# A hybrid S5 / gated-DeltaNet encoder step: tables behind the first block, the second block's norm in two operations, the steps' tiles placed anew

## The chip, the core and the metric

The kernel runs on one NeuronCore of one Trainium2 chip. A core has five engines that run in parallel, each through its own list of instructions and strictly in that order: TensorE (PE, matrix products, with PEld for its weight loads), VectorE (DVE), ScalarE (ACT), GpSimd (POOL) and SyncE (SP). They wait for each other through semaphores. Transfers between HBM and the on-chip memory SBUF are issued by SP, ACT or POOL and carried out by 16 DMA engines. Products land in PSUM, a small memory of eight banks, from which ACT or DVE copies them out ("evicts" them).

The metric is the device time of one execution in microseconds (us); less is better.

## The reference

Two layers work on one prompt of 2048 rows and on eight sample streams of 16 rows each, 2176 rows of width 1024 in all. Each layer is a normalisation, a modulation from a conditioning vector `c`, a mixer, and a gated residual:

```python
cs = jax.nn.silu(c)
for i in range(DEPTH):
    mod = cs @ w_ada[i] + b_ada[i]
    shift, scale, gate = jnp.split(mod[:, None, :], 3, axis=-1)
    h = rms_norm(x, norm_g[i]) * (1.0 + scale) + shift
    out = s5_branch(h, ...) if i == 0 else gdn_branch(h, ...)
    x = x + gate * out
y = rms_norm(x, final_g)
```

The change lies in layer 0, the S5 mixer:

```python
proj = h @ w_in                        # 1024 -> 2048
u, z = jnp.split(proj, 2, axis=-1)
# 64 groups of 16 channels, each with 64 complex states:
#   x_t = Abar x_{t-1} + Bbar u_t,   y_t = Re(C x_t)
# Abar = exp(lambda * step), Bbar = (Abar - 1) / lambda * B
y = gelu(y + d * u)
y = y * sigmoid(y @ w_glu + b_glu) * silu(z)
out = y @ w_out
```

Everything is float32. To keep that precision on PE at a higher rate, an operand is split into a high half (rounded to the fp32r format) and a low half (the rest), and each product is made of three: high x high, high x low, low x high.

## The kernel before, in words

**Blocks.** Rows are held transposed: features on the 128 partitions, in 8 slices of 128, and rows as columns. The columns are cut into 8 blocks of 272 (256 of the prompt, 16 of the samples). The first phase takes each block through norm, modulation, split into halves (`hh`, `hl`) and the first half of `w_in`: 8 column tiles `cb`, each 8 slices x 3 = 24 products into one PSUM tile (`pd`), evicted by ACT (`ev`) and stored to `u_d`. The modulated block itself is stored to `h0_d`, because the second half of `w_in` is applied to it later.

**The first block.** At the start nothing is loaded yet, so the order is written out by hand. A wrapper `Engine` with `ordered = True` issues each instruction of an engine behind the one before it in the program; it is set for T (PE), V (DVE) and S (ACT) from line 378 to line 423, and for SY (SP). The loop over slices (385 to 408) makes, for slice `k`, the products that give its shift and scale (`first_mod`), splits two column tiles of the weights (`split_raw`), normalises the slice, adds the products of an earlier slice (`first_prod`) and scales the slice (`first_scale`). Behind the loop, lines 409 to 421, stand the products of slices 6 and 7, the square of the second block (`norm_sq(xt1, xsq)`), two evictions, the split of the weight tiles 6 and 7, the second block's norm and modulation (`apply_mod(1, ..., True)`), column tiles 6 and 7 of the first block, and the other evictions. `norm_sq` squares half a block on ACT and adds it up on DVE; `norm_r` sums over partitions with a product by a constant matrix (`ms`), takes the root on ACT and the reciprocal on DVE; `norm_mul` multiplies the whole block by it.

**Everything else is placed by a planner.** An instruction that is not ordered is put into its engine's list by the framework, which simulates the program and takes what is ready; `later(list)` and `tc.issue_after(...)` make it keep an instruction behind given ones on the same engine. `after` is the last DVE instruction of the hand-written part. Not ordered are the step coefficients on 32 columns (430 to 505: `dexp`, the sine, the repeated squarings `unit_square` in `transitions`, which also makes `abar`, `nr`, `ni`), the tables of the steps (`s5_tables`, in 8 parts, on POOL with some rows on DVE at lines 555 and 557, loads and stores on POOL's queue), and the rotation tables (`rot_factors`, `rot_table`, on DVE, stored through ACT's queue). Before the change `s5_tables` parts are issued in blocks 1 to 6 with no `later`, the rotation tables in blocks 0 to 5 behind `after`.

**The loop over blocks** (589 to 618) computes block `j` and, at `cb == 4`, modulates block `j + 1`, loads block `j + 2` and issues the tables that are due; at `cb == 7` it normalises block `j + 2`. Its products are ordered on PE only for `j == 1`.

**The steps.** The second phase (631 to 937) takes 16 steps, each for two of the state pairs, with the scan on DVE. Between them PE is filled with `z_block`: 24 products of the second half of `w_in`, evicted by ACT as `evz` out of two PSUM buffers. In each step `n` such blocks are issued (3 or 4), and behind the first of them ACT copies the states (`s5_states`). The tiles of the steps come from three memory pools, `b3`, `b2` and `b1`, opened in this order on the memory that the first phase leaves.

Of the kernel before, what the change touches and what calls it, by code (L numbers as in the profile page):

```python
# [10 lines left out]
F32 = mybir.dt.float32  # L11
# [24 lines left out]


PWO, BBO, BDO, CCO, SPW = 0, 54, 118, 246, 310
TABLES = {1: (0, 1), 2: (2,), 3: (3,), 4: (4, 5), 5: (6,), 6: (7,)}
NATT = [(0, 512), (512, 512), (1024, 384), (1408, 384), (1792, 384)]  # L40


# [12 lines left out]
def kernel(ctx: ExitStack, tc: tile.TileContext, I, O, upto="Z"):  # L55
# [156 lines left out]
    def ks(t, n=KC):  # L212
        return [t[:, k] for k in range(n)]
# [13 lines left out]
    def split_x(nm, xt, hf):  # L227
        a = hp.tile([P, 4, NCH], F32R, tag="hh", name=f"hh{nm}_{hf}")
        b = hp.tile([P, 4, NCH], F32R, tag="hl", name=f"hl{nm}_{hf}")
        spl["i"] = [S.copy(a, xt).ins, V.tensor_sub(b, xt, a.bitcast(F32)).ins]  # L230
        return ks(a, 4), ks(b, 4)

    with ExitStack() as pa:
# [11 lines left out]
            ld = SY.dma_start(xt, I["xT"][j])  # L245
            return xt, ld.ins

        def norm_sq(xt, sqs=None):
            acc = sp1.tile([P, 2, NCH], F32, tag="acc", name="acc")
            for hf in range(2):  # L250
                sq = sqs[:, 4 * hf:4 * hf + 4] if sqs else sp1.tile([P, 4, NCH], F32, tag="sq", name="sq")
                xh = xt[:, 4 * hf:4 * hf + 4]
                S.activation(sq, xh, AF.Square)
                V.tensor_add(sq[:, 0:2], sq[:, 0:2], sq[:, 2:4])
                V.tensor_add(acc[:, hf], sq[:, 0], sq[:, 1])
            return acc
# [16 lines left out]
        def norm_x(xt, fold=False):  # L273
            return norm_mul(xt, norm_r(norm_sq(xt), fold=fold))

        def apply_mod(j, xt, first=False):
            xs = xt[:, :, NPC:NCH].rearrange("p k (q h) -> p k q h", h=2)
            V.tensor_mul(xs, xs, bc(gs0[:, :, 1:9], 3, 2))
            V.tensor_add(xs, xs, bc(modT[:, 0:8, 1:9], 3, 2))
            hl = []  # L280
            for hf in range(2):
                k4 = range(4 * hf, 4 * hf + 4)
                if not first:
                    for k in k4:
                        xk = xt[:, k, 0:NPC]
                        S.activation(xk, xk, AF.Identity, scale=gs0[:, k, 0:1], bias=modT[:, k, 0:1])
                    hl.append(split_x(j, xt[:, 4 * hf:4 * hf + 4], hf))
                    continue
                a, b = (hp.tile([P, 4, NCH], F32R, tag=t, name=f"{t}{j}_{hf}") for t in ("hh", "hl"))
                S.copy(a[:, :, NPC:NCH], xt[:, 4 * hf:4 * hf + 4, NPC:NCH])  # L290
                for i, k in enumerate(k4):
                    xk = xt[:, k, 0:NPC]
                    S.activation(a[:, i, 0:NPC], xk, AF.Identity, scale=gs0[:, k, 0:1], bias=modT[:, k, 0:1])
                    V.tensor_scalar(xk, xk, gs0[:, k, 0:1], modT[:, k, 0:1], op0=ALU.mult, op1=ALU.add)
                V.tensor_sub(b, xt[:, 4 * hf:4 * hf + 4], a.bitcast(F32))
                hl.append((ks(a, 4), ks(b, 4)))
            (h0, l0), (h1, l1) = hl
            if j < 7:
                nc.scalar.dma_start(h0_d[j], xt)
            return h0 + h1, l0 + l1  # L300

        SY.ordered = True
        fold = sst.tile([P, 9], F32, name="fold")
# [81 lines left out]
        for k in range(KC):  # L385
            if k == 2:
                SY.dma_start(lsd, I["ls"])
                SY.dma_start(lre, I["lr"])
                SY.dma_start(lim, I["li"])
            nwt = load_mod(k + 1) if k < 7 else None  # L390
            if k == 6:
                xt1 = load_x(1)[0]
            mA = first_mod(k, wt)
            nraws = [load_raw(cb) for cb in ((2 * k + 2, 2 * k + 3) if k < 2 else (6, 7) if k == 6 else ())]
            for w in raws if k < 7 else ():
                split_raw(*w)
            V.tensor_mul(xcur[:, k], xcur[:, k], r0)
            if k == 1:
                first_prod(0)
            elif k == 2:  # L400
                first_prod(1, range(2))
            elif k == 3:
                first_prod(1, range(2, 6))
            elif k > 3:
                first_prod(k - 2)
            first_scale(k, mA)
            if k < 7:
                wt, raws = nwt, nraws
        first_prod(6)
        first_prod(7)  # L410
        acc1 = norm_sq(xt1, xsq)
        first_copy(0)
        first_copy(1)
        for w in raws:
            split_raw(*w)
        hnext = apply_mod(1, norm_mul(xt1, norm_r(acc1)), True)
        for cb in range(2, 8):
            if cb > 5:
                pd0 += [psd.tile([P, NCH], F32, tag="d", name=f"pd0_{cb}")]
                mm3(pd0[cb], ks(wu_hi[cb]), ks(wu_lo[cb]), *hcur)  # L420
            first_copy(cb)
        after = [V.last]
        T.ordered = V.ordered = S.ordered = False
        nc.scalar.dma_start(h0_d[0], xcur)
# [56 lines left out]
        def transitions():  # L481
            V.tensor_copy(gk[:, :, 0, :], un)
            for _ in range(3):
                unit_square(gk[:, :, 0, :], gk[:, :, 0, :])
            for lv in range(1, 7):
                unit_square(gk[:, :, lv, :], gk[:, :, lv - 1, :])
            V.tensor_mul(a8, gk[:, :, 0, :], bc(rN, 1, 2))

            V.tensor_mul(abar, un, bc(mag, 1, 2))
            e1, e2, den, xr = ta  # L490
            V.tensor_mul(e1, lre, lre)
            V.tensor_mul(e2, lim, lim)
            V.tensor_add(e1, e1, e2)
            V.reciprocal(den, e1)
            V.tensor_scalar(xr, abar[:, 0], -1.0, None, op0=ALU.add)
            V.tensor_mul(e1, xr, lre)
            V.tensor_mul(e2, abar[:, 1], lim)
            V.tensor_add(e1, e1, e2)
            V.tensor_mul(nr, e1, den)
            V.tensor_mul(e1, abar[:, 1], lre)  # L500
            V.tensor_mul(e2, xr, lim)
            V.tensor_sub(e1, e1, e2)
            V.tensor_mul(ni, e1, den)

        transitions()

        def s5_tables(part):

# [80 lines left out]
        for j in range(8):  # L589
            hh, hl = hcur  # L590
            T.ordered = j == 1
            for cb in range(8):
                if cb == 4:
                    if j < 7:
                        hcur = apply_mod(j + 1, xnext) if j else hnext
                    V.ordered = S.ordered = j == 0
                    if j < 6:
                        xn, xl = load_x(j + 2)
                        if j == 0:
                            xnext = norm_x(xn)  # L600
                    V.ordered = S.ordered = False
                    SY.ordered = False
                    for part in TABLES.get(j, ()):
                        s5_tables(part)
                    with later(after):
                        if j == 0:
                            rot_factors()
                        for i in range(3 * j, min(3 * j + 3, 16)):
                            rot_table(i)
                if j > 0:  # L610
                    ps = psd4.tile([P, NCH], F32, tag="d", name=f"pd{j}_{cb}")
                    i_ = mm3(ps, ks(wu_hi[cb]), ks(wu_lo[cb]), hh, hl)
                    store_u(j, cb, ps)
                if cb == 7 and 0 < j < 6:
                    xnext = norm_x(xn)
                if j > 1 and cb % 3 == 1:
                    with later([xl, i_]):
                        ada.pop(0)()
# [11 lines left out]

    with ExitStack() as pb:
        ps5 = pb.enter_context(ExitStack())
        b3 = ps5.enter_context(tc.tile_pool(reuse_waits="tile", name="b3", bufs=3))
        b2 = ps5.enter_context(tc.tile_pool(reuse_waits="tile", name="b2", bufs=2))
        b1 = ps5.enter_context(tc.tile_pool(reuse_waits="tile", name="b1", bufs=1))
        ps_t = pb.enter_context(tc.tile_pool(reuse_waits="tile", name="ps_t", bufs=1, space=PSUM))
        ps_b = pb.enter_context(tc.tile_pool(reuse_waits="tile", name="ps_b", bufs=1, space=PSUM))
        ps_y = pb.enter_context(tc.tile_pool(reuse_waits="tile", name="ps_y", bufs=2, space=PSUM))
# [178 lines left out]

        def s5_y(b, pl):
            toe, u, cx, x = toes[b], us[b], cxs[b], xss[b][0]
            y = b2.tile([P, 2, NCH], F32, tag="y", name=f"y{b}_{pl}")  # L820
            pys = [ps_y.tile([P, NCH], F32, tag="y", name=f"py{b}_{2 * pl + i}") for i in range(2)]
            for i in range(2):
                T.matmul(pys[i], lhsT=toe[:, 2 * pl + i], rhs=u[:, 2 * pl + i], start=True, stop=False)
# [61 lines left out]
        for b in range(16):  # L885
# [32 lines left out]
            n = 4 if b % 2 == 0 and b < 11 or b == 15 else 3  # L918
            for i in range(n):
                z_block()  # L920
                if i == 0:
                    s5_states(b, t, xo)
                if i == 1 and len(zh) < 14 and zst["n"] >= 8 * (len(zh) // 2):
                    next_half()
# [1329 lines left out]
```

## Time and profile before

| what | value |
|---|---|
| median of three runs | 2116.36 us (2115.76 to 2120.4) |
| the profiled execution, its own time | 2108.51 us |
| its span, first to last instruction | 2106.8 us |
| mean granted PE clock | 0.992 of full speed |
| PE busy | 2049.0 us, 97% |
| DVE busy | 1484.4 us, 70% |
| ACT busy | 1013.8 us, 48% |
| POOL busy | 489.5 us, 23% |
| HBM traffic | 168 GB/s over the span |

The profile is of one execution. Each row of a timeline gives the start and the duration of an instruction in us, its engine, its line in the kernel (L70 is the wrapper of the ordered instructions), the operation, the written and read tiles, and, in brackets, how long the engine had been idle before it and what released it. The granted clock is the share of PE's full speed that the hardware allowed in that stretch.

### The profile page before, as it was taken

What the parts mean: (1) busy time and instruction counts of PE and PEld (TensorE: products, weight loads), DVE (VectorE), ACT (ScalarE), POOL (GpSimd) and SP (SyncE); (2) the same over time, 40 slices, a digit from 0 to 9 for tenths busy, and PEclk for the clock granted to TensorE, in tenths of its full rate; (3) what the DMA queues carried; (4) which work ended last, traced back from release to release, by engine and by line L of the source; (5) the groups of instructions that cost most, each with busy time, mean ns of one, the idle gap of its engine ahead of it and who ended that gap; (6) DMA issues with size and microseconds to landing.
All of it is one profiled execution on the core that took longest, in us unless ns stands there. A gap on an engine that the chain in (4) does not pass through costs nothing.

```text
span 2106.8 us, 41346 instructions
## 1 busy us (share of the span) xinstructions
PE 2049.0 (97%) x15473; PEld 1826.3 (87%) x15473; DVE 1484.4 (70%) x3401; ACT 1013.8 (48%) x2426; POOL 489.5 (23%) x742
## 2 busy tenths in 40 slices
PE   7899999999999999999999999999999899999998
PEld 5798888888889999999888879899987688888886
DVE  7988558788667544556665669688556788888885
ACT  3544335555455444445665422342223656666663
POOL 3089210000113322221100010100011344444430
PEclk9899999999999999999999999999999999999999
DMA  7687846666477433326565212653455944444432
GB/s 290 253 291 282 288 148 203 193 188 194 138 246 253 137 110 110 114 92 243 153 198 172 80 54 75 165 149 103 137 169 198 302 148 136 132 138 150 149 115 71
DMA packets 318069, 356.34 MB, mean 169 GB/s; under 512 B 88906, under 2 KB 261466, under 8 KB 315052
## 3 DMA queue, kind: packets, MB, share of 16 engines
q1 hardware_dynamic: 186700, 242.62, 36.1%
q10 hardware_dynamic: 126944, 98.57, 14.2%
q0 software_dynamic: 4224, 12.51, 1.7%
q8 instruction: 122, 2.00, 0.4%
q14 instruction: 79, 0.65, 0.1%
HBM read 229.20 MB, written 124.41 MB: 168 GB/s over the span
## 4 chain that ended last, share of the span: by engine, by line
PE 82%; DVE 7%; DMA 6%; ACT 3%; issue 1%; POOL 1%; SPq 0%; ACTq 0%; DVEq 0%; POOLq 0%
PE pdz L70 8%; PE epo L70 7%; PE pc L152 5%; PE pc L153 5%; PE pc L154 5%; PE pz L154 3%; PE pz L153 3%; PE pz L152 3%; PE py L70 3%; PE po L152 3%; PE po L154 3%; PE po L153 3%; PE pd L152 2%; PE pd L154 2%; PE pd L153 2%; PE pg L154 2%
## 5 line engine op out<-in xcount | busy, mean ns | idle before, releaser
L152 PE MATMUL pc<-h1h,wdh 128*128 128x512 f32 (+1 forms) x600 | 216.5, 361 | 0.4 <-ACT pb L1549 0.4
L153 PE MATMUL pc<-h1l,wdh 128*128 128x384 f32 (+1 forms) x600 | 214.8, 358 | 0.2 <-POOL h1l L1500 0.2
L154 PE MATMUL pc<-h1h,wdl 128*128 128x384 f32 (+1 forms) x600 | 214.9, 358 | 0.0
L1560 DVE SCALAR_TENSOR_TENSOR ac<-pb,convw,ac 128x384 f32<-128x384 f32 (+3 forms) x288 | 163.6, 591 | 3.3
L152 PE MATMUL po<-gh,woh 128*128 128x272 f32 x512 | 145.3, 290 | 2.4 <-ACT gh L1084 1.7
L154 PE MATMUL po<-gh,wol 128*128 128x272 f32 x512 | 147.4, 289 | 0.0
L153 PE MATMUL po<-gl,woh 128*128 128x272 f32 x512 | 147.1, 289 | 0.2
L70 PE MATMUL pdz<-hhz,wzh 128*128 128x272 f32 x448 | 131.9, 294 | 4.4 <-ACT evz L70 4.4
L153 PE MATMUL pg<-yl,wgh 128*128 128x272 f32 x448 | 129.8, 290 | 0.0
L70 PE MATMUL pdz<-hhz,wzl 128*128 128x272 f32 x448 | 129.5, 289 | 0.0
L154 PE MATMUL pg<-yh,wgl 128*128 128x272 f32 x448 | 129.3, 289 | 0.0
L70 PE MATMUL pdz<-hlz,wzh 128*128 128x272 f32 x448 | 129.2, 288 | 0.0
L152 PE MATMUL pg<-yh,wgh 128*128 128x272 f32 x448 | 129.0, 288 | 0.0
L152 PEld LDWEIGHTS pc<-h1h,wdh 128*128 128x128 f32 x600 | 112.6, 188 | 12.7 <-issue 1.7
L153 PEld LDWEIGHTS pc<-h1l,wdh 128*128 128x128 f32 x600 | 112.7, 188 | 10.5 <-issue 0.8
L154 PEld LDWEIGHTS pc<-h1h,wdl 128*128 128x128 f32 x600 | 112.6, 188 | 10.1 <-issue 0.8
L152 PE MATMUL pd<-hh,wuh 128*128 128x272 f32 x384 | 112.1, 293 | 0.0
L70 PE MATMUL epo<-w2h,ohi 128*128 128x512 f32 x272 | 111.5, 410 | 0.0
L154 PE MATMUL pd<-hh,wul 128*128 128x272 f32 x384 | 110.8, 289 | 0.0
L153 PE MATMUL pd<-hl,wuh 128*128 128x272 f32 x384 | 110.1, 287 | 0.0
L70 PE MATMUL epo<-w2l,ohi 128*128 128x512 f32 x272 | 107.6, 395 | 1.8 <-DMA w2l<-w2l_d 1.7
L1081 POOL TENSOR_TENSOR zt<-zt,sz 128x272 f32<-128x272 f32 x64 | 61.3, 964 | 206.0 <-ACT sz L1080 205.1
(647 smaller groups left out, 6338.5 us busy)
## 6 DMA issues: line engine op xcount, KB each, us to landing
wa<-in_w_ada SPq DMA_DIRECT2D x32, 512.0 KB
wdr<-in_w_in SPq DMA_DIRECT2D x24, 512.0 KB
u_d<-ev ACTq DMA_DIRECT2D x64, 136.0 KB
u<-u_d SPq DMA_DIRECT2D x16, 544.0 KB
z_d<-evz ACTq DMA_DIRECT2D x64, 136.0 KB
y_d<-y ACTq DMA_DIRECT2D x32, 272.0 KB
zt<-z_d SPq DMA_DIRECT2D x64, 136.0 KB
xa<-in_xT SPq DMA_DIRECT2D x8, 1088.0 KB
```

Source lines behind the costliest of these rows:

```text
L70: i_ = f(*a, **kw)
L152: T.matmul(ps, lhsT=w_hi[k], rhs=x_hi[k], start=(k == 0), stop=False)
L153: T.matmul(ps, lhsT=w_hi[k], rhs=x_lo[k], start=False, stop=False)
L154: i_ = T.matmul(ps, lhsT=w_lo[k], rhs=x_hi[k], start=False, stop=(k == n - 1))
L1081: G.tensor_mul(zt, zt, sz)
L1560: V.scalar_tensor_tensor(o, src(j), convw[:, b, j:j + 1], o, op0=ALU.mult, op1=ALU.add)
```

## The change

Four things are done.

1. *Tables and coefficients.* `TABLES` puts the parts in pairs into blocks 2 to 5, and their issue, like that of the rotation factors and tables (one block later than before), stands under `later(after)`. The last part of `transitions` becomes `step_factors`, also under `later(after)`. The squarings stay where they were.
2. *The second block's norm.* Its square is made in the loop of the first block, one half in slice 6 and one in slice 7; ACT's table for the root is loaded ahead of it. The split of the weight tiles 6 and 7, the sum over partitions and the root come ahead of the last slice's products.
3. *Its modulation, in two operations.* `second_block` replaces the normalisation of the whole block and the scaling: one DVE operation multiplies by the reciprocal and by the scale, one ACT operation adds the shift and rounds to the high half, and one DVE operation adds the shift and subtracts the high half. ACT then adds the shift once more, in place, for the copy that is stored. Evictions stand between the halves, and the products of column tiles 6 and 7 ahead of it all.
4. *The steps.* Pool `b1` is opened ahead of `b3` and `b2`, the `y` tile moves into it, and in step 15 the copies of the states stand behind the second `z_block` instead of the first.

```diff
-TABLES = {1: (0, 1), 2: (2,), 3: (3,), 4: (4, 5), 5: (6,), 6: (7,)}
+TABLES = {2: (0, 1), 3: (2, 3), 4: (4, 5), 5: (6, 7)}
...
-        def norm_sq(xt, sqs=None):
-            acc = sp1.tile([P, 2, NCH], F32, tag="acc", name="acc")
-            for hf in range(2):
+        def norm_sq(xt, sqs=None, acc=None, part=range(2)):
+            acc = sp1.tile([P, 2, NCH], F32, tag="acc", name="acc") if acc is None else acc
+            for hf in part:
...
+        def second_block(xt, r, copies):
+            xs = xt[:, :, NPC:NCH].rearrange("p k (q h) -> p k q h", h=2)
+            V.tensor_mul(xs, xs, bc(r[:, NPC:NCH].rearrange("p (q h) -> p q h", h=2), 1, KC))
+            V.tensor_mul(xs, xs, bc(gs0[:, :, 1:9], 3, 2))
+            V.tensor_add(xs, xs, bc(modT[:, 0:8, 1:9], 3, 2))
+            a, b = ([hp.tile([P, 4, NCH], F32R, tag=t, name=f"{t}1_{hf}") for hf in range(2)] for t in ("hh", "hl"))
+            for hf in range(2):
+                for i in range(4):
+                    k = 4 * hf + i
+                    xk = xt[:, k, 0:NPC]
+                    V.scalar_tensor_tensor(xk, r[:, 0:NPC], gs0[:, k, 0:1], xk, op0=ALU.mult, op1=ALU.mult)
+                    S.activation(a[hf][:, i, 0:NPC], xk, AF.Identity, bias=modT[:, k, 0:1])
+                S.copy(a[hf][:, :, NPC:NCH], xt[:, 4 * hf:4 * hf + 4, NPC:NCH])
+                for cb in copies[hf]:
+                    first_copy(cb)
+            for hf in range(2):
+                for i in range(4):
+                    k = 4 * hf + i
+                    V.scalar_tensor_tensor(b[hf][:, i, 0:NPC], xt[:, k, 0:NPC], modT[:, k, 0:1],
+                                           a[hf][:, i, 0:NPC].bitcast(F32), op0=ALU.add, op1=ALU.subtract)
+                V.tensor_sub(b[hf][:, :, NPC:NCH], xt[:, 4 * hf:4 * hf + 4, NPC:NCH],
+                             a[hf][:, :, NPC:NCH].bitcast(F32))
+            for k in range(KC):
+                xk = xt[:, k, 0:NPC]
+                S.activation(xk, xk, AF.Identity, bias=modT[:, k, 0:1])
+            nc.scalar.dma_start(h0_d[1], xt)
+            return [ks(t[0], 4) + ks(t[1], 4) for t in (a, b)]
...
             V.tensor_mul(xcur[:, k], xcur[:, k], r0)
+            if k == 6:
+                S.preload_act_table_set("sqrt_and_others")
+            if k > 5:
+                acc1 = norm_sq(xt1, xsq, acc1 if k == 7 else None, (k - 6,))
...
+        for w in raws:
+            split_raw(*w)
         first_prod(6)
+        r1 = norm_r(acc1)
         first_prod(7)
-        acc1 = norm_sq(xt1, xsq)
         first_copy(0)
         first_copy(1)
-        for w in raws:
-            split_raw(*w)
-        hnext = apply_mod(1, norm_mul(xt1, norm_r(acc1)), True)
-        for cb in range(2, 8):
-            if cb > 5:
-                pd0 += [psd.tile([P, NCH], F32, tag="d", name=f"pd0_{cb}")]
-                mm3(pd0[cb], ks(wu_hi[cb]), ks(wu_lo[cb]), *hcur)
-            first_copy(cb)
+        for cb in range(6, 8):
+            pd0 += [psd.tile([P, NCH], F32, tag="d", name=f"pd0_{cb}")]
+            mm3(pd0[cb], ks(wu_hi[cb]), ks(wu_lo[cb]), *hcur)
+        hnext = second_block(xt1, r1, ((2, 3), (4, 5)))
+        first_copy(6)
+        first_copy(7)
         after = [V.last]
...
+        def step_factors():
             V.tensor_mul(abar, un, bc(mag, 1, 2))
...
         transitions()
+        with later(after):
+            step_factors()
...
-                    for part in TABLES.get(j, ()):
-                        s5_tables(part)
                     with later(after):
-                        if j == 0:
+                        for part in TABLES.get(j, ()):
+                            s5_tables(part)
+                        if j == 1:
                             rot_factors()
-                        for i in range(3 * j, min(3 * j + 3, 16)):
+                        for i in range(max(0, 3 * j - 3), min(3 * j, 16)):
                             rot_table(i)
...
+        b1 = ps5.enter_context(tc.tile_pool(reuse_waits="tile", name="b1", bufs=1))
         b3 = ps5.enter_context(tc.tile_pool(reuse_waits="tile", name="b3", bufs=3))
         b2 = ps5.enter_context(tc.tile_pool(reuse_waits="tile", name="b2", bufs=2))
-        b1 = ps5.enter_context(tc.tile_pool(reuse_waits="tile", name="b1", bufs=1))
...
-            y = b2.tile([P, 2, NCH], F32, tag="y", name=f"y{b}_{pl}")
+            y = b1.tile([P, 2, NCH], F32, tag="y", bufs=2, name=f"y{b}_{pl}")
...
-                if i == 0:
+                if i == b // 15:
                     s5_states(b, t, xo)
```

The branch of `apply_mod` that served the second block alone is removed with it.

More of the change, by code (lines that the diff above doesn't have):

```diff
@@ L274, in norm_x, with apply_mod @@
             return norm_mul(xt, norm_r(norm_sq(xt), fold=fold))
-        def apply_mod(j, xt, first=False):
+        def apply_mod(j, xt):
             xs = xt[:, :, NPC:NCH].rearrange("p k (q h) -> p k q h", h=2)
@@ L281, in apply_mod @@
             for hf in range(2):
[L282 to L291, printed above, removed]
+                for k in range(4 * hf, 4 * hf + 4):
                     xk = xt[:, k, 0:NPC]
[L293 to L296, printed above, removed]
+                    S.activation(xk, xk, AF.Identity, scale=gs0[:, k, 0:1], bias=modT[:, k, 0:1])
+                hl.append(split_x(j, xt[:, 4 * hf:4 * hf + 4], hf))
             (h0, l0), (h1, l1) = hl
```

## The prediction

> **What bounds the kernel now.** I read the page first, then the waits, then the timeline of each engine up to 140 us, and last the stretch round the sixteenth S5 step.
>
> ```profile
> span 2106.8 us, 41346 instructions
> PE 2049.0 (97%) x15473; PEld 1826.3 (87%) x15473; DVE 1484.4 (70%) x3401; ACT 1013.8 (48%) x2426; POOL 489.5 (23%) x742
> ```
>
> PE lacks only 2106.8 - 2049.0 = 57.8 us, so a change pays where PE waits or where its clock is down. The waits of PE, for the first 80 us and then from there to 560 us (total, times, longest):
>
> ```profile
> PE ms L70 <- DVE acc L70: 10.2, 3, 7.9
> PE pd L70 <- ACT ev L70: 4.7, 1, 4.7
> PE psc L70 <- DVE mA L70: 3.7, 2, 2.7
> ...
> PE pb L70 <- issue: 0.5, 1, 0.5
> PE pdz L70 <- ACT evz L70: 0.4, 1, 0.4
> ```
>
> The 7.9 us are the wait for the very first input. The other large ones fall between 47 and 77 us, where the first block of 272 columns ends and the second is made ready; from 80 to 560 us PE waits 0.9 us in all. PE's own rows (start, duration, in brackets the idle time before):
>
> ```profile
> 46.83 0.29 PE L70 MATMUL pd<-hl,wuh 128*128 128x272 f32 x1
> 46.95 0.28 PE L70 MATMUL pd<-hh,wul 128*128 128x272 f32 x1
> ...
> 77.05 0.59 PE L70 MATMUL pd<-hh,wuh 128*128 128x272 f32 x1 [4.70 <-ACT ev L70]
> ...
> 81.52 0.39 PE L70 MATMUL pd<-hl,wuh 128*128 128x272 f32 x1
> 81.75 0.29 PE L70 MATMUL pd<-hh,wul 128*128 128x272 f32 x1
> ```
>
> Before the stalls one product starts about 0.125 us after the last (46.95 - 46.83), behind them 0.227 us (81.75 - 81.52). So a stall is paid twice, as idle time and in clock. The stretches round the first stall show the same (busy time of PE, PEld, DVE, ACT, POOL, then granted clock, DMA share, GB/s):
>
> ```profile
> 44.00:48.00 4.00, 3.24 (x34) 2.52 (x26) 3.53 (x15) 0.60 (x1) 3.59 (x12) 1.00 0.01 2
> 48.00:52.00 4.00, 2.04 (x13) 2.04 (x14) 4.00 (x19) 0.43 (x2) 3.53 (x11) 0.88 0.01 2
> ```
>
> What PE waits for is DVE. DVE works in order, and table work that the steps want 200 us later stands in that order ahead of the second block and waits for its own buffers:
>
> ```profile
> 53.94 0.46 DVE L555 TENSOR_TENSOR ca<-sp 128x288 f32<-128x288 f32 x1 [1.75 <-DMA ca_d<-ca]
> ...
> 60.74 0.83 DVE L555 TENSOR_TENSOR ca<-sp 128x288 f32<-128x288 f32 x2 [2.09 <-DMA ca_d<-ca]
> ...
> 66.14 1.84 DVE L70 RECIPROCAL r<-r 128x272 f32<-128x272 f32 x1
> ...
> 73.25 0.41 DVE L70 TENSOR_SCALAR x<-x,gs,modT 128x256 f32<-128x256 f32 x1
> ```
>
> **The head, part by part.** First what PE must still do after 47.1 (46.95 + 0.125) before block 1 may start, at full clock: the scale product of slice 7 (0.51), slices 6 and 7 of the first block at 18 x 0.125 = 2.25 each, columns 6 and 7 at 48 x 0.125 = 6.0, and the norm product, 0.92 by the chain of waits (start, duration):
>
> ```profile
> 104.37 0.92 PE ms L70 x4
> 105.29 0.38 PE pd L152 x3
> ```
>
> The sum is 11.9, so block 1 can start at 59.0 at best, against 77.05. Whether DVE and ACT allow it is the real question. The rows for it, of the timelines and of the groups on DVE between 36 and 77 us:
>
> ```profile
> 43.28 0.51 PE L70 MATMUL psc<-fold,mA 128*128 128x9 f32 x4
> ...
> 55.54 1.10 ACT L70 ACTIVATE xsq<-x 128x1088 f32<-128x1088 f32 x1
> ...
> 57.37 0.72 DVE L70 TENSOR_TENSOR xsq<-xsq 128x544 f32<-128x544 f32 x1
> ...
> 60.12 1.28 ACT L70 ACT_TABLE_LOAD   x1
> ...
> 72.55 2.07 ACT L70 ACTIVATE hh<-x,modT,gs 128x256 fp32r<-128x256 f32 x4
> ```
>
> ```profile
> L555 DVE TENSOR_TENSOR cat<-sp 128x288 f32<-128x288 f32 x8 | 3.6, 453 | 1.1 <-POOL sp L454 1.1
> L557 DVE TENSOR_TENSOR ca<-ca,cat 128x288 f32<-128x288 f32 x8 | 3.6, 447 | 0.0
> L555 DVE TENSOR_TENSOR ca<-sp 128x288 f32<-128x288 f32 x8 | 3.4, 459 | 3.8 <-DMA ca_d<-ca 3.8
> ...
> L70 DVE TENSOR_TENSOR wul<-wr,wuh 128x1024 fp32r<-128x1024 f32 x2 | 2.4, 1219 | 0.0
> ```
>
> *The two halves of the second block's square* now stand in slices 6 and 7, each ahead of that slice's scaling: 1.10 on ACT, then about 1.1 on DVE (0.72, and a sum of half that size). Their input has landed, since the DMA share is 0.01 from 44 us on. The preloaded table (1.28) stands ahead of the first square, so ACT ends it near 43.7, and DVE takes slice 6's scales near 44.8 instead of 43.8. What is queued behind it on DVE is the low half and the copy that PE's next scale product reads; that copy is there by 46.4, and PE has other products until 47.1. The cover is about 0.7 us; if it is gone, PE stands by what is missing, up to the 2.2 of both halves.
>
> *Weights 6 and 7* are split ahead of the norm instead of after it (2.4 on DVE), ending near 52.7. Then come the reciprocal (1.84) until 54.5, three narrow operations (0.7 together) until 55.2, and eight fused multiplies of 256 columns. The trace has no fused operation of this shape. The scalar form took 0.41; at a pace of 0.33, as such rows overlap, eight are 2.7, and at the 0.453 of the two-tensor rows of 288 columns above, without overlap, 3.6. I take 2.7, since the elements are those of the 0.41 row.
>
> So the low halves begin near 58, and the first four are there at 59.5. ACT makes its eight high halves beside them at 0.51 each (2.07 for four), with four evictions between, until 60.6, just ahead of the low halves that read them. The eight more ACT passes for the stored copy (4.1 us) and its store then lie beside the 24 us of block 1's products; without that cover they would delay the next square by as much.
>
> *Fillers.* The squarings of the rotation (L463 to L474) are not put behind the first block. Four rounds of 11 passed between 47 and 77, one start 0.1 us after the other:
>
> ```profile
> 71.77 0.18 DVE L463 TENSOR_TENSOR sm<-gk 128x32 f32<-128x32 f32 x1
> 71.88 0.18 DVE L464 TENSOR_TENSOR sm<-gk 128x32 f32<-128x32 f32 x1
> ```
>
> In the 12 us that are left, 44 x 0.1 x 12/30 = 1.8 us. I put block 1's start at 61.0, between 59.0 and 64.3 (59.0 + all 4.4 of the fillers + 0.9 of slower multiplies): a gain of 77.05 - 61.0 = 16.0, between 12.7 and 18.0. Of the 20 slow products behind 77.05 (20 x 0.102 = 2.0) I keep 0.7, as a shorter stall remains: gain 1.3, bounds 0 and 2.0.
>
> [...]
>
> *The seam to block 2.* Its square started at 80.73 and its products at 105.29, 24.6 us later, with no idle time and nothing to spare:
>
> ```profile
> 80.73 1.11 ACT L70 ACTIVATE sq<-x 128x1088 f32<-128x1088 f32 x1
> ```
>
> Now it starts near 67, after the stored copy and two evictions. Block 1 ends near 61 + 24 + 1.9 (two norm products) = 86.9, and 67 + 24.6 = 91.6: a stall of up to 4.7. But the rotation tables that shared DVE with it, which was full (27.10 of 28 us, below), now stand a block later. I charge 1.0, bounds 0 and 4.7.
>
> **What moves.** The 24 table rows above (10.6 us on DVE), their four stores, the POOL operations and small loads that feed them go behind the first block, two parts to a block from the third on. The rotation tables go one block on, with their stores on ACT's queue. PE covers this if DVE has room:
>
> ```profile
> 77.00:105.00 28.00, 27.95 (x201) 27.67 (x201) 27.10 (x114) 16.60 (x31) 2.02 (x3) 0.92 0.72 264
> ...
> 133.00:161.00 28.00, 28.00 (x220) 25.16 (x212) 25.48 (x51) 11.54 (x24) 27.13 (x64) 1.00 0.84 279
> ```
>
> One part is 10.6 / 2 = 5.3 us of DVE. Cost 0, down to -10 (the first rival). The small loads that POOL no longer issues at the start: 0. The new order of the steps' memory pools: 0, since PE waits at their start only the 0.5 us above.
>
> **Step 15.** Its state copies go behind the second gate block on ACT:
>
> ```profile
> 557.86 0.39 ACT L70 COPY evz<-pdz 128x272 f32<-128x272 f32 x1 [2.27 <-PE pdz L70]
> ...
> 565.23 1.24 ACT L70 COPY xs<-xo 64x510 f32<-64x510 f32 x2 [0.45 <-DVE xo L70]
> ...
> 566.93 0.59 PE L70 MATMUL pdz<-hhz,wzh 128*128 128x272 f32 x1 [3.10 <-ACT evz L70]
> ```
>
> The second eviction can then run near 561 (557.86 and a block of 24 x 0.125), so the 3.10 go, and with them some twelve slow products (1.2). Late next is the third eviction, behind the copies until 566.9, when PE ends its fourth block anyhow. Gain 4.0 of 4.3; 0 at least, if the next phase's weights hold PE instead.
>
> **The sum** is made against the profiled execution (span 2106.8, 2108.51 with what lies around it): 16.0 + 1.3 - 1.0 + 4.0 = 20.3 less. The median shown, 2116.36, lies 7.85 above that execution; I carry the difference over: 2116.36 - 20.3 = 2096.0.
>
> **Rivals.** *Half is given back by DVE.* The seam costs 4.7 and 2.0 of clock, and two blocks with a part more overrun 28 us (25.48 + 5.3 = 30.8, 2.8 each): 20.3 + 1.0 - 6.7 - 5.6 = 9.0 gained, time 2107.4. For it: 27.10 of 28 busy. Against it: from 80 us on PE waited for none of this. [...]
>
> ```profile
> 139.93 2.29 POOL L454 TENSOR_TENSOR sp<-pt,pt 128x4 f32<-128x4 f32 x1
> ...
> 139.61 2.54 DVE L270 TENSOR_TENSOR x<-x,r 128x2176 f32<-128x2176 f32 x1
> ...
> 230.41 0.55 POOL L558 DMA_DIRECT2D ca_d<-ca  x1 [5.37 <-DVE ca L557]
> ```
>
> *The second block is not ready earlier after all.* The squares in slices 6 and 7 and the fillers hold up the first block by what they save, and only step 15 is left: 2112.4. Against it: DVE's own waits of 1.75 and 2.09 go with the tables. *Slower: norm products stand in PE's order ahead of late sums.* If one part's DVE rows (5.3) stand between a sum and its norm product, PE stands as long and loses 1.2 in clock, in blocks 2 to 5: 26 lost, time 2122. It decides from 20.3 / 4 = 5.1 us per block. For it: pairs of parts. Against it: the last store, at 230.41, is 55 us ahead of the steps, so table work can slip behind sums.
>
> **How the numbers follow.** Forecast 0.64, half given back 0.19, not ready earlier 0.09, slower 0.08. About 0.2% (4.2 us) is what can be told from no change: faster 0.83, same 0.09, slower 0.08. The best case is 18.0 + 2.0 + 4.3 = 24.3, time 2092; the three times shown before spread from 2115.76 to 2120.4, so I put the lower end 3 lower, at 2089. The upper end, 2109, lies just past the first rival. The forecast's own range is 2089 to 2102.
>
> **What would show it.** Right: block 1's first product near 61 us, clock 1.00 from 32 us on, no table row on DVE before it, no wait of 3.1 in step 15. Wrong: PE waiting for a norm sum or a low half after 86 us; DVE above 27 of 28 in three blocks running; PE idle at the start of the steps.

## The result, and the profile after

The changed kernel takes 2100.62 us (median of four runs, 2098.2 to 2104.91); the kernel before, beside it on the same chip, takes 2117.99 (2115.76 to 2120.4). The ratio is 0.992, interval 0.9897 to 0.9943: 17.4 us less, where 20.3 were forecast. The time forecast, 2096.0, is 4.6 below the one measured, inside the range of 2089 to 2109. One of the twelve timed runs of e2 below took 5103.11 us and is left out of its figures.

The two profiled executions don't show this difference in their spans: the one shown of before was shorter than all its timed runs, and the one of after the longest of four. So what follows compares stretches of the traces, not their ends. The page of the changed kernel gives its span:

```profile
span 2103.2 us, 41357 instructions
```

The waits of PE up to 110 us (total, times, longest):

```profile
PE ms L70 <- DVE acc L70: 8.4, 2, 8.1
PE pd L152 <- ACT hh L230: 3.4, 1, 3.4
PE pd L70 <- DVE hl L70: 2.8, 4, 2.0
PE ms L263 <- DVE acc L70: 1.7, 1, 1.7
...
PE psc L70 <- DVE mA L70: 1.2, 2, 1.0
PE pd L153 <- DVE hl L230: 0.6, 1, 0.6
```

The wait of 4.7 for an eviction is gone, and that for `mA` fell from 3.7 to 1.2. But three entries are new: for the sum of a norm (L263), and for the high and the low half of block 2 (L230); and the wait for a low half of block 1 has grown from 1.2 to 2.8. PE's own rows show where they stand (start, duration, in brackets the idle time before):

```profile
59.81 0.39 PE L70 MATMUL pd<-hh,wuh 128*128 128x272 f32 x1
62.23 0.39 PE L70 MATMUL pd<-hl,wuh 128*128 128x272 f32 x1 [2.03 <-DVE hl L70]
...
70.67 0.72 PE L263 MATMUL ms<-acc,onesd 128*128 128x272 f32 x2 [1.73 <-DVE acc L70]
...
89.62 1.08 PE L70 MATMUL ms<-acc,onesd 128*128 128x272 f32 x4
94.09 0.78 PE L152 MATMUL pd<-hh,wuh 128*128 128x272 f32 x4 [3.39 <-ACT hh L230]
```

Blocks are counted from 0, so block 1 is the second one. It begins at 59.81 with a single product; with the next at 62.23 it is as far as if it had started at 62.1, against 77.05 before. It ends at 89.6. Block 2 then comes 3.39 us late. By stretches (busy time of PE, PEld, DVE, ACT, POOL, then granted clock, DMA share, GB/s):

```profile
77.00:105.00 28.00, 23.99 (x162) 23.05 (x162) 28.00 (x80) 13.05 (x25) 3.51 (x9) 0.88 0.67 247
105.00:133.00 28.00, 28.00 (x222) 24.35 (x221) 18.34 (x38) 11.88 (x25) 20.11 (x54) 1.00 0.87 299
133.00:161.00 28.00, 28.00 (x220) 25.16 (x212) 24.26 (x53) 11.56 (x23) 20.77 (x50) 1.00 0.92 313
```

The stretch from 77 to 105 us ran at a full PE (27.95 of 28) before. Now DVE is full there (28.00), PE lacks 4.0 us, and the clock is down to 0.88. From 105 us on PE is full, and DVE has room. The norm of block 2 starts with its square on ACT; then come DVE's rows:

```profile
68.00 1.12 ACT L70 ACTIVATE sq<-x 128x1088 f32<-128x1088 f32 x1
...
71.71 1.57 DVE L579 TENSOR_TENSOR ca<-sp 128x288 f32<-128x288 f32 x4
...
73.81 0.72 DVE L70 TENSOR_TENSOR sq<-sq 128x544 f32<-128x544 f32 x1
74.46 0.46 DVE L581 TENSOR_TENSOR ca<-ca,cat 128x288 f32<-128x288 f32 x1
...
75.48 0.43 DVE L70 TENSOR_TENSOR acc<-sq 128x272 f32<-128x272 f32 x1
...
80.63 1.84 DVE L70 RECIPROCAL r<-r 128x272 f32<-128x272 f32 x1
```

The rows of `ca`, which the program issues in block 2, stand here during block 1, between the square, its sum and the reciprocal. In the steps, PE's waits between 300 and 600 us are now these and one of 0.3; before there were 4.4 for the gate blocks' evictions (`evz`, under `pdz`) and 1.3 ahead of `pg`:

```profile
PE pg L70 <- DVE wgl L140: 0.7, 1, 0.7
PE pg L70 <- ACT evz L70: 0.5, 1, 0.5
```

### The profile page after: what moved, and what is told of

Its sections match the earlier page's. It is cut to its first block, busy times and chain, and to the rows that moved or that the text cites. A ratio compares the mean times of both kernels' runs of the same rounds, so it can differ in the third digit from the quotient of the medians.

```text
span 2103.2 us, 41357 instructions
## 1 busy us (share of the span) xinstructions
PE 2047.4 (97%) x15473; PEld 1825.1 (87%) x15473; DVE 1483.6 (71%) x3409; ACT 1015.1 (48%) x2434; POOL 489.1 (23%) x742
## 4 chain that ended last, share of the span: by engine, by line
PE 85%; DVE 6%; DMA 5%; ACT 3%; issue 1%; POOL 0%; SPq 0%; ACTq 0%; DVEq 0%; POOLq 0%
PE pdz L70 8%; PE epo L70 7%; PE pc L152 5%; PE pc L153 5%; PE pc L154 5%; PE pz L154 3%; PE pz L153 3%; PE pz L152 3%; PE po L154 3%; PE py L70 3%; PE po L153 3%; PE po L152 3%; PE pd L152 2%; PE pg L154 2%; PE pg L152 2%; PE pg L153 2%
```

## The experiments

Each kernel is compared with the kernel before on the same chip. Beside the ratio, the table has landmarks of the trace in us, read off the view by tile, whose rows give the first and the last start of a group. For the changed kernel these rows are

```profile
L152 PE MATMUL pd<-hh,wuh x384: 282/288/428, 94.1 to 265.3; 128*128 128x272 f32 x192
```

```profile
L70 PE MATMUL pdz<-hh,wzh x64: 283/288/400, 266.0 to 297.4; 128*128 128x272 f32 x64
```

```profile
L70 PE MATMUL pg<-yh,wgh x64: 283/287/396, 576.4 to 601.6; 128*128 128x272 f32 x64
```

"Block 2" is the first start of the first, "end of blocks" the last start of the second, "steps" the distance from there to the first `pg`, with which the next phase begins.

| kernel | block 2 | end of blocks | steps | first `pg` | median, us | ratio to before, interval |
|---|---|---|---|---|---|---|
| before, as shown | 104.9 | 304.5 | 285.4 | 589.9 | 2117.99 | 1 |
| c0, before again | 105.8 | 305.4 | 286.8 | 592.2 | 2115.86 | 1.0004 (0.9989 to 1.0018) |
| after, as shown | 94.1 | 297.4 | 279.0 | 576.4 | 2100.62 | 0.992 (0.9897 to 0.9943) |
| c1, after again | 93.7 | 296.8 | 279.0 | 575.8 | 2099.04 | 0.9921 (0.9905 to 0.9937) |
| e1 | 90.8 | 291.1 | 278.8 | 569.9 | 2094.32 | 0.9903 (0.988 to 0.9925) |
| e2 | 87.7 | 309.5 | 278.3 | 587.8 | 2114.39 | 0.9987 (0.9971 to 1.0003) |
| e3 | 93.8 | 295.6 | 283.6 | 579.2 | 2106.04 | 0.9952 (0.9936 to 0.9968) |
| e4 | 102.5 | 303.0 | 279.0 | 582.0 | 2110.1 | 0.9972 (0.9957 to 0.9987) |
| e5 | 96.6 | 299.2 | 285.8 | 585.0 | 2112.71 | 0.9983 (0.9971 to 0.9994) |
| e6 | 86.9 | 286.7 | 278.9 | 565.6 | 2091.78 | 0.9886 (0.9867 to 0.9905) |
| e7 | 92.7 | 294.2 | 282.7 | 576.9 | 2107.44 | 0.9968 (0.9954 to 0.9982) |
| e8 | 105.0 | 304.6 | 283.2 | 587.8 | 2113.67 | 0.9988 (0.9978 to 0.9998) |
| e9 | 90.7 | 293.4 | 279.0 | 572.4 | 2101.12 | 0.9928 (0.991 to 0.9945) |

**c0 and c1: both kernels again.** No edit.

> The kernel before, unchanged, for a trace beside those of the others. The profile shown before is of an execution of 2108.51 us, while the timed ones took 2115.76 to 2120.4. Theory 1: the start is the same in every execution (block 1's first product near 77 us, PE's wait of 3.1 in step 15), and the 7 to 10 us between executions arise behind step 15, where weights come by DMA; then this trace has block 1 near 77 and its extra time behind 560 us. Rival: executions differ by an even stretch of everything, and every mark of this trace lies some 0.4% later.

> The changed kernel, unchanged. Forecast of the prediction: 20 us less than before, ratio 0.990. By the two traces at hand: block 1's products from 60 us, block 2's from 94 to 96 us, 11 us ahead of the kernel before at step 15's last products. Ratio 0.990 to 0.994. If only the profiled executions counted, 3.6 us less, 0.998.

The two executions of each kernel agree within 1 us up to the end of the blocks (e3 and e7, with the same code up to there as after and c1, widen that to 3.2). The two of before are 0.1 apart at the last high product of the steps' gate blocks (588.1 and 588.2), 2.3 at the first `pg`, and 6.6 at the end. Most of this scatter lies behind the first `pg`, where the change touches nothing. From there to the start of the kernel's last group of products the thirteen traces take 1507.4 to 1523.1 us. The three with the whole head of before (before, c0, e8) are the shortest there, with 1507.4 to 1512.0. The medians don't bear this out as an effect of the change: they fall by 17.4 us, and the traces show 15.8 up to the first `pg` (below). What makes this scatter isn't located; the landmarks before it carry the reading.

**e1: the tables, and the rotation's factors and tables, behind block 2's split** instead of behind the first block.

```diff
+                    if j == 1:
+                        after = spl["i"]
                     with later(after):
                         for part in TABLES.get(j, ()):
```

> The changed kernel, with the tables and the rotation factors issued behind the split of block 2 instead of behind the hand-written part. Theory: PE's waits and the low clock between 70 and 110 us come from table and rotation rows that stand in DVE's order within block 2's norm; then block 2's products start near 88 instead of 94 to 96 us, and the kernel is 5 to 8 us faster than the changed one. Rival: the seam is set by ACT (stored copy, evictions that wait for their stores); then block 2 starts within 2 us of 94 and the time is the same.

PE's rows at the seam, and the stretch of 77 to 105 us, of this kernel:

```profile
90.82 0.74 PE L152 MATMUL pd<-hh,wuh 128*128 128x272 f32 x3
```

```profile
77.00:105.00 28.00, 28.00 (x221) 26.85 (x221) 23.78 (x54) 16.38 (x30) 15.54 (x33) 1.00 0.86 298
```

```profile
76.90 1.84 DVE L70 RECIPROCAL r<-r 128x272 f32<-128x272 f32 x1
```

The reciprocal comes at 76.90 instead of 80.63, block 2 follows block 1 without a gap (at 90.8, as block 1 itself lost clock, 0.78 and 0.79 over 8 us; see the last section), PE is full and the clock 1.00. The blocks end 6.3 us earlier, and the medians differ by 4.7 to 6.3 (2094.32 against 2099.04 and 2100.62), at the lower end of the 5 to 8 expected. The intervals of the ratios overlap, so the reading rests on the traces. The seam's stall came from the work held back here, which DVE took too early; which part of it, e9 tells.

**e2: all of it behind block 2's split**, the squarings and the step coefficients too.

```diff
-        transitions()
-        with later(after):
-            step_factors()
...
+                    if j == 1:
+                        after = spl["i"]
+                        with later(after):
+                            transitions()
+                            step_factors()
```

> As the run before it, and the squarings of the rotation and the step coefficients behind block 2's split too, so that DVE has only the two blocks until then. Theory: the squarings cost block 1 about 1.8 us (block 1's second product near 60.4 instead of 62.2 us) and block 2 another 2 to 3; 8 to 11 us faster than the changed kernel, unless the tables are then late for the steps at 265 us (PE idle there). Rival: the squarings lie in DVE's idle time; no difference to the run before it.

Block 2 follows without a gap, at 87.7, but now PE waits later. PE's waits from 110 to 560 us:

```profile
PE abT L70 <- DVE abt L725: 10.2, 2, 8.0
PE pd L152 <- ACT ev L326: 3.7, 2, 3.0
PE ada L188 <- DVE modT L198: 2.3, 1, 2.3
```

```profile
279.01 0.42 DVE L723 TENSOR_TENSOR abt<-sp 128x256 f32<-128x256 f32 x1
```

`abt`, which the steps need, is made from the tables. Here the last `ca` row starts on DVE at 278.63, and the first `abt` comes right behind it. The last table goes out at 279.4, against 230.4 before and 249.1 in e6. So the room of 55 us that the prediction read off the last store is used up, and PE waits 8.0 for the first `abt` and 2.2 for a later one. The other 6.0 of the 16 us of waits lie in the blocks and are not traced further.

**e6: e1, with the squarings behind the first block's hand-written order**, so that they don't fill the gaps of block 1's norm.

```diff
-        transitions()
         with later(after):
+            transitions()
             step_factors()
```

> The kernel of e1 (tables behind block 2's split) with the squarings of the rotation also put behind the first block's hand-written order, so that they no longer fill gaps of the second block's norm. Theory (the squarings cost block 1 the 1.8 us of the prediction): no 128x32 row on DVE between 47 and 60 us, PE's wait for block 1's first low half falls from 2.0 to 1.2 us or less, block 1 and block 2 start 1 to 2 us earlier than in e1, and the time is 1 to 2 us less than that of e1 (about 2093). Rival (what is put behind the first block fills DVE in block 2's norm in its turn, as in the changed kernel, and makes the step coefficients late, as in e2): block 2 starts at 91 us or later, waits for abT show before 310 us, and the time is 2096 or more.

PE's waits up to 110 us, and its rows:

```profile
PE pd L70 <- DVE hl L70: 1.8, 3, 1.2
...
PE ms L263 <- DVE acc L70: 0.5, 1, 0.5
```

```profile
59.99 0.39 PE L70 MATMUL pd<-hl,wuh 128*128 128x272 f32 x1 [1.23 <-DVE hl L70]
```

Block 1's first low half is used at 59.99 instead of 62.33 in e1, block 2 starts at 86.9, and the time is 2091.78, the best of all: 24 us below before (0.9886 x 2116.16 = 2092.0). The squarings cost 2.3, where 1.8 was estimated. The median is 2.5 below that of e1, with intervals that overlap; in the traces block 2 starts 3.9 earlier, and up to 1.7 of that is the clock that e1 lost in block 1 (last section). The `abT` wait of e2 does not come, so two holds of different length (squarings behind the first block, tables behind block 2's split) are better than one for all.

**e9: e1 with the rotation not held.** The eight table parts stay behind block 2's split; the rotation's factors and first tables stand as in the changed kernel.

```diff
                         for i in range(max(0, 3 * j - 3), min(3 * j, 16)):
                             rot_table(i)
+                    if j == 1:
+                        after = spl["i"]
```

> The kernel of e1, but with the rotation's factors and its first three tables behind the first block only, as changed; the eight table parts and the later rotation tables stay behind block 2's split. Theory (the ca rows of the two table parts fill DVE in block 2's norm): block 2's first product comes at 90 to 92 us as in e1, without a wait for hh, and the time is within 2 us of e1's. Rival (the rotation's rows do it): block 2 waits 2 to 4 us for hh as in the changed kernel and starts at 93 to 94 us, and the time is within 2 us of the changed kernel's. In between: both do.

The place is as the theory had it: block 2 at 90.7 and no wait for its halves, so the `ca` rows made the stall and not the rotation's. The time is not: 2101.12, not within 2 us of e1's 2094.32, though the intervals of the two ratios overlap. PE's waits from 88 to 270 us show part of the reason:

```profile
PE pd L152 <- ACT ev L326: 2.2, 1, 2.2
```

One eviction comes 2.2 late in a later block, and the blocks end 2.3 behind e1. The other 4.5 of the two medians are not located.

**e4 and e5: the two halves of the head apart.** e4 is the changed kernel with tables, coefficients and rotation placed as before; e5 is the kernel before with only these placed as changed.

```diff
-TABLES = {2: (0, 1), 3: (2, 3), 4: (4, 5), 5: (6, 7)}
+TABLES = {1: (0, 1), 2: (2,), 3: (3,), 4: (4, 5), 5: (6,), 6: (7,)}
...
-        with later(after):
-            step_factors()
+        step_factors()
```

> The changed kernel with the tables, the step coefficients and the rotation tables placed as before; the second block's norm stays within the first block, split in two operations. Theory (both parts are needed, since DVE fills the gaps of the hand-written order with table rows and waits for their stores): rows of ca stand on DVE between 40 and 62 us, block 1's first product comes 4 to 12 us later than in the changed kernel, at 64 to 72 us, and the ratio to the kernel before is 0.994 to 0.998. Rival (the early norm alone makes the head, and the tables only fill idle DVE time): block 1's first product stays within 1 us of 60, block 2 comes at 88 to 91 us as no rotation table shares its norm, and the ratio is 0.990 or less.

> The kernel before with only the tables, the step coefficients and the rotation tables placed as changed; second block's norm and step 15 as before. Theory (the table rows and their store waits in the head, 10.6 and 4.9 us on DVE before block 1, stood on the path): block 1's first product comes at 63 to 67 us in place of 77, and the ratio to the kernel before is 0.993 to 0.996. Rival (the rows filled time in which DVE waited for ACT and PE anyway): block 1 starts behind 72 us, and the ratio is 0.998 or more.

In e4 DVE stands in the middle of the first block, at a table's buffer, with the scales of a slice queued behind it:

```profile
57.09 0.83 DVE L578 TENSOR_TENSOR ca<-sp 128x288 f32<-128x288 f32 x2 [2.68 <-DMA ca_d<-ca]
```

PE's waits up to 110 us, of e4 and then of e5:

```profile
PE psc L70 <- DVE mA L70: 6.1, 2, 4.9
```

```profile
PE pd L152 <- ACT hh L230: 3.5, 1, 3.5
```

e4 starts block 1 at 72.67, just past the 64 to 72 expected, and its second product waits until 75.21; it gains 1.5 at the end of the blocks (304.5 - 303.0) and ends at 0.9972, most of it from the steps (279.0 against 285.4). The early norm is of little use while table rows stand in DVE's order. e5 starts block 1 at 65.43, as expected, but gains only 5.3 at the end of the blocks (304.5 - 299.2); its ratio, 0.9983, misses the 0.993 to 0.996 expected. The 3.5 is the seam's wait. Rows of `ca` stand in the norm of block 2 here too, from 75.3 us on; that they make this wait is not shown by a run of its own. So the tables are the larger part, and the two gains add up to 6.8, near the 7.1 of the changed kernel (304.5 - 297.4): neither kernel shows that one part is worthless without the other.

**e3, e7 and e8: the steps.** e3 has the state copies of step 15 back in their old place, e7 the old pools, and e8 is the kernel before with the new pools alone.

```diff
-                if i == b // 15:
+                if i == 0:
```

```diff
-        b1 = ps5.enter_context(tc.tile_pool(reuse_waits="tile", name="b1", bufs=1))
         b3 = ps5.enter_context(tc.tile_pool(reuse_waits="tile", name="b3", bufs=3))
         b2 = ps5.enter_context(tc.tile_pool(reuse_waits="tile", name="b2", bufs=2))
+        b1 = ps5.enter_context(tc.tile_pool(reuse_waits="tile", name="b1", bufs=1))
...
-            y = b1.tile([P, 2, NCH], F32, tag="y", bufs=2, name=f"y{b}_{pl}")
+            y = b2.tile([P, 2, NCH], F32, tag="y", name=f"y{b}_{pl}")
```

> The changed kernel with the state copies of step 15 back behind its first gate block; all else as changed. Theory (the wait was worth what it took): in step 15 PE waits about 3.1 us again for the second gate eviction, the products of the next phase start about 4 us later than in the changed kernel, and the median is 4.0 us longer, which is a ratio to the kernel before of about 0.994 in place of 0.992. Rival (something behind step 15 held PE anyway): the 3.1 us come back but another wait of the same size between 560 and 600 us goes, and the ratio stays within 0.001 of 0.992.

> The changed kernel with the steps' memory pools and the y tiles placed as before. Measure: PE's time from the last product of block 7 (the last pdz of hh) to the first product of the next phase (the first pg), which was 285.4, 286.8 and 285.8 us in the three profiles with old pools and old step 15, 283.6 with new pools and old step 15, and 279.0 in those with both new. Theory (the pool order is worth 1.8 to 3.2 us at the steps' end, against the prediction's 0): the stretch is 281 to 282 us, PE waits 1 to 3.5 us there for evz, and the median is 2 to 3 us above the changed kernel's. Rival (the pool order is worth nothing by itself, as predicted; the waits for evz go with the late step 15): the stretch is 279.0 and the ratio that of the changed kernel, 0.992.

> The kernel before with only the steps' memory pools and the y tiles placed as changed. Theory (the pool order is worth 1.8 to 3.2 us at the steps' end): the stretch from block 7's last product to the first pg is 283 to 284 us, the wait of the first pg products for evz falls to 0.5, the 3.1 of step 15 stays, and the ratio is 0.998 to 0.999. Rival (worth nothing by itself): 285 to 287 us and a ratio within 0.001 of 1.

PE's waits from 300 to 600 us, of e3, of e7 and of e8:

```profile
PE pdz L70 <- ACT evz L70: 3.1, 1, 3.1
```

```profile
PE pg L70 <- ACT evz L70: 2.2, 1, 2.2
PE py L70 <- ACT y L70: 1.7, 1, 1.7
```

```profile
PE pdz L70 <- ACT evz L70: 3.5, 2, 3.1
...
PE pg L70 <- ACT evz L70: 0.5, 1, 0.5
```

The late state copies are worth 283.6 - 279.0 = 4.6 us of the steps, near the 4.0 forecast (with the old pools 286.0 - 282.7 = 3.3). The pools are worth 3.7 with them (282.7 - 279.0) and 2.8 without (the mean of 285.4, 286.8 and 285.8 less 283.2). Neither hides the other; the three traces behind that mean differ by 1.4 among themselves. In e7's trace what is late is seen on ACT: the last evictions of `y` and `evz` stand behind splits and casts that wait for transfers. The first split of these weights (`wgh`) starts at 560.0 in e7 and at 570.5 in the kernel before, but at 571.3 in the changed kernel and at 582.1 in e8: some 11.5 us later with the new pools, both times. Why the order of the pools moves it is not shown.

```profile
560.03 1.04 ACT L138 CAST wgh<-wgr 128x1024 fp32r<-128x1024 f32 x1 [1.57 <-DMA wgr<-in_w_glu]
...
571.73 1.10 ACT L1053 CAST yh<-yc 128x1088 fp32r<-128x1088 f32 x1 [1.70 <-DMA yc<-y_d]
```

The median of e7 lies 8.4 above c1's and that of e3 7.0, more than the 3.7 and 4.6 of the trace. The intervals of the ratios are wide enough for it (their nearest ends are 3.6 us apart for e7 and touch for e3), but the rest isn't located.

## Why the prediction held, point by point

Against 16.3 forecast (16.0 + 1.3 - 1.0) the head gained less: the blocks end at 304.8 in the mean of the shown before, c0 and e8, and at 296.0 in the mean of after, c1, e3 and e7, which have the same code up to there. That is 8.8. The steps gained more: 7.0 (286.0 to 279.0) against 4.0. So 15.8 are seen up to the first `pg`, and the medians' 17.4 agree within their interval of 12 to 22. So the head gained 7.5 less than forecast and the steps 3.0 more: that the sum came near is in part luck, two misses of opposite sign.

*What bounds the kernel, and the start of block 1: right.* With no table row ahead of it and the square in slices 6 and 7, block 1 starts as if at 62.1 (forecast 61.0, bounds 59.0 and 64.3). Of these 15.0 us the tables alone bring 11.6 (e5: 65.43) and the early norm alone some 2 (e4: 75.1, by its second product). The sizes that were off are small:

```profile
57.52 2.85 DVE L70 SCALAR_TENSOR_TENSOR x<-r,gs,x 128x256 f32<-128x256 f32 x7
60.38 1.67 DVE L70 SCALAR_TENSOR_TENSOR hl<-x,modT,hh 128x256 fp32r<-128x256 f32 x4
```

The prediction has the low halves from 58 without the squarings, and e6, which holds these back, has them from 58.14. With 1.8 for the squarings that is 59.8; they begin at 60.38, and PE waits 2.03. A fused multiply goes at 2.85 / 7 = 0.41, between the 0.33 taken and the 0.453 of the upper bound, which is 0.6 for the eight. The squarings were 2.3, not 1.8, by PE's rows in e6 and e1.

*Clock behind block 1's start: better than put.* The 2.03 us stall cost no clock in this execution, 1.00 from 60 to 68 us; see the last section.

*The norm sum within block 1: not costed.* PE stands 1.73 ahead of `ms` at 70.67. The square starts on ACT at 68.00, behind an eviction that had waited 1.71 for the store of its buffer; DVE waits 1.36 for that square, and only 0.37 of other rows lie between its two operations on it, none of them a `ca` row. In e6 the wait is 0.47. This is the mechanism of the slower rival, a norm product in PE's order ahead of a late sum, at one place and for 1.7 instead of four times 5.1.

*The step that failed is the seam.* The prediction charged 1.0 of a possible 4.7, because "the rotation tables that shared DVE with it" now stand a block later, and put the moved tables at 0. It took the block in which a part is issued for the block in which it runs. Issued is not run: the parts are kept only behind the first block's hand-written part, and the planner was free to put what was ready into DVE's order from there on. So 6.36 us of `L579` and 3.01 of `L581`, the `ca` rows, fell between 64 and 94 us:

```profile
64.00:94.00 30.00, 6.36 (x15) 1.00 0.76 271
```

```profile
64.00:94.00 30.00, 3.01 (x7) 1.00 0.76 271
```

(Stretch of those two lines' instructions alone, first L579, then L581.) The rotation's rows did not move out of it either: two of their lines, L470 and L471, take 2.84 there. By e9 it is the `ca` rows that cost. The square started at 68.00, near the 67 forecast, but the products came 26.1 later (94.09 - 68.00). Before it was 24.2 by the same kind of row (104.92 - 80.73); the prediction's 24.6 goes by the chain of waits.

```profile
104.92 0.74 PE L152 MATMUL pd<-hh,wuh 128*128 128x272 f32 x3
```

The whole charge is the stall of 3.39 and 0.62, and the clock behind it. In the two stretches of 12 us that hold it, the clock is 0.80 and 0.91, which is 12 x 0.20 + 12 x 0.09 = 3.5 at most, as they hold idle time too. By PE's rows, products start 0.227 us apart from 95.94 to 102.00, instead of 0.125, which is 6.06 x (1 - 0.125 / 0.227) = 2.7. Together that makes 6.7 to 7.5 instead of 1.0, and e1 gets 6.3 of it back with two lines. That is 5.7 to 6.5 over the charge. With a start 1.1 late and 1.73 for the norm sum, less the 0.7 of clock that was not lost, it comes to 7.8 to 8.6, near the 7.5 that the head lacks.

```profile
88.00:100.00 12.00, 7.99 (x43) 7.05 (x42) 12.00 (x41) 7.71 (x14) 0.98 (x2) 0.80 0.43 165
100.00:112.00 12.00, 12.00 (x88) 11.01 (x88) 10.12 (x31) 5.79 (x12) 4.91 (x13) 0.91 0.55 172
```

```profile
96.56 0.43 PE L152 MATMUL pd<-hh,wuh 128*128 128x272 f32 x1
96.79 0.43 PE L153 MATMUL pd<-hl,wuh 128*128 128x272 f32 x1
```

*Half given back by DVE:* the rival named this place, a seam of 4.7 and 2.0 of clock, and was near with its 6.7. Its other half, 5.6 for two overfull blocks, didn't come: PE is full from 105 to 161 us. The sign "DVE above 27 of 28" shows in one stretch, not three. But another sign of being wrong did come, PE waiting for a low half after 86 us (0.62 at 95.94), and of the signs of being right the clock of 1.00 failed at the seam.

*Step 15: right,* 4.0 forecast, 4.6 by e3. *The pools: put at 0, measured 2.8 to 3.7.* The prediction looked for their effect at the start of the steps, where PE waits little; it lies at their end, in the wait of `pg` for `evz`: 1.3 in the kernel before as shown, 3.5 in c0, and 0.5 in e8 with the new pools.

*The second block not ready earlier:* excluded, by block 1's start.

## What to carry to other kernels

Where a planner fills idle engines, "issued later" only sets the earliest point: ask what keeps each group back, and put the hold behind the last work that must not share the engine (here two lines, 6 us in the trace), but no longer than its first reader allows (10 us of waits for `abt` in e2). An early start of one block is worth little while something else stands in the same engine's order, so look for what ends the wait after the one removed, and cost it with the clock that can fall behind it (0.78 and 0.79 behind e1's stall of 2.03 us, 1.00 behind the same stall in the changed kernel). And a late order of buffers is to be looked for at the end of the phase that uses them, not only at its start.

## What the runs showed of the hardware

The same stall does not cost the same clock. In the changed kernel, in c1 and in e1 PE stands 2.03 us at the same place. Stretches of 4 us behind it, after first, then e1:

```profile
60.00:64.00 4.00, 1.97 (x13) 1.55 (x12) 4.00 (x14) 3.93 (x12) 0.00 (x0) 1.00 1.02 317
64.00:68.00 4.00, 3.84 (x31) 3.84 (x31) 3.78 (x33) 2.29 (x8) 3.15 (x16) 1.00 0.90 300
```

```profile
60.00:64.00 4.00, 1.97 (x8) 1.76 (x9) 4.00 (x15) 3.94 (x12) 0.00 (x0) 0.78 0.98 312
64.00:68.00 4.00, 4.00 (x28) 4.00 (x27) 3.11 (x23) 2.07 (x6) 2.98 (x16) 0.79 0.92 298
```

The clock stays at 1.00 in one and falls to 0.78 and 0.79 in the other, up to 1.7 us of lost time over 8 (4 x 0.22 + 4 x 0.21). Three more kernels have the same stall of 2.03: e3 and e7 keep 1.00 behind it, e9 falls to 0.84 and 0.73. And c1 and e3, which kept their clock here, lost it behind the shorter stalls of 1.87 and 1.79 for the norm sum (0.72 and 0.65 from 72 to 76 us), where the changed kernel with 1.73 and e7 with 1.53 kept 1.00. So the prediction's 0.7 kept of 2.0 was neither right nor wrong as one number: by these six traces it looks like a chance, two times in six. What decides it in one execution, no run here shows, and the length of the stall alone doesn't: behind 1.87 it was lost in c1, where behind 2.03 it had been kept.
